# Moving the sub-norm's partition sum on GpSimd, and four smaller steps, in a hand-ordered decoder trunk

## Chip, cores and metric

The kernel runs on one core of one Trainium2 chip. The metric is the device time of one execution in microseconds, the median of several runs. TensorE (PE, with its weight loads as PEld), VectorE (DVE), ScalarE (ACT), GpSimd (POOL) and SyncE (SP) each work through a queue of their own, in order, and wait for each other with semaphores. DMAs are issued from SP, POOL and ACT.

## The reference

One layer of a decoder trunk, 1024 tokens of width 2048, all in float32. Cut to what matters here:

```python
hn = rmsnorm(h, norm_mix_g[i])
proj = hn @ w_in[i]
sb_q, sb_k, sb_v, sb_g, df_q, df_k, df_v, df_g = jnp.split(proj, split_at, axis=-1)
sb_out = stick_breaking_attention(...)          # 8 heads of 128: "SB"
dq, dk = partial_rope(df_q), partial_rope(df_k) # 8 heads of 2 x 64: "DF"
df_out = differential_attention(dq, dk, df_v, lam)
df_out = rmsnorm(df_out, subln_g[i], SUBLN_EPS) * (1.0 - lambda_init)   # the sub-norm, over 128 columns of a head
mixed = concat([sb_out * silu(sb_g), df_out * silu(df_g)])
h = h + mixed @ w_out[i]
gate = sigmoid(rmsnorm(h, norm_ple_g[i]) @ w_ple_gate[i])
h = h + gate * (p[i] @ w_ple_proj[i])
return rmsnorm(h, norm_final_g)
```

## The kernel before

Everything lies transposed: features on the 128 partitions, tokens along the free axis, in two halves of 512 tokens. Every large product is made with three matmuls, because an operand is split into a high part (a cast to fp32r, on ACT) and a low part (what is left, a subtraction on DVE): high x high, high x low and low x high. In the profile the high casts are lines such as L202, L517, L682, L684, L802 on ACT, and the low parts L198, L522, L688, L690, L816 on DVE.

The work comes in this order:

1. **The v and gate columns** of the input projection, as block products with seven multiplications (operands A11, A12, S1 to S4, A22, class `Seven`). One `prod` is 12 matmuls, and after each one `step` is called, which counts `slot` up by one. A step splits one more piece of weights (`whigh` L802, `wlow` L816), then does what is in `soon`, then calls `chore`, then takes up to two operand splits out of the list `xq` whose slot has come (three if more than eight wait, four after the change in slots of the new set `rush`). In `chore` there is also the dictionary `joint`: at given slots it sums the squares of x over partitions (`total`, GpSimd, L1152), takes the root (`root`, ACT, L1157 and L1158) and refines it in three DVE steps (`refined`, L1166, L1168, L1170), once for each token half.
2. **The q and k columns and both attentions.** For each token half (half 1 first, then half 0) and each of 16 heads, in the order DF, SB, DF, SB, ..., `unit` makes 96 matmuls, three for each of its 32 ticks. After each tick `side.tick()` runs those steps of a list sorted by due time that have come due. All of attention is in that list: scores, softmax or stick-breaking, transposes of the weights (`turn`, L498), their splits (`parts`: high part L516 and L517, low part L521 and L522), the products with v (`mix`, L540 and L543 to L545), the sub-norm of a DF head, and the turning of q and k of the head that was just projected. `side.later(dt, fn)` puts a step in dt ticks after the present one. Numbers come from the table `TICK`; heads 15 and 7 of each half have entries of their own under `mid_` (half 1) and `end_` (half 0).
3. **The output projection and the gate product**, again `Seven` (`op`), `gprod` being the version that calls `step` after each 12 of its 24 matmuls; `gate_loads` loads operands of the gate product and puts their splits into `xq`.

The orders of PE, DVE and ACT are the program's order, written by hand. The orders of SP and POOL are made by the scheduler when the kernel is built, from the program's order and a simulated timeline.

The sub-norm of a DF head, after its last product with v: `squared` (Square on ACT, L572, and the product with the sub-norm's gain on DVE, L573) three ticks after that `mix`, the sum over partitions on GpSimd (`partition_all_reduce`, L579) a tick and a half later, and at a fixed tick `norm`: Ln and Exp on ACT (L589, L590), four DVE steps (L593 to L596).

In the first half (half 1) a unit of an SB head looks like this, by the ticks of that unit: the last `mix` of the DF head before it at tick 6; Square at 9 and the partition sum at 10; the last addition of k's rotary turn (L1583) at 11, the four casts of k (L1560, L1564) at 14, its low parts (L1571) at 16 and 17, the casts into k's ends (L1578) at 18; meanwhile the first transposes of another SB head at tick 11 and their `mix` at 17, the next one at 23; Ln of the DF head's sub-norm at 26.

Of the kernel before, what the change touches and what calls it, by code (L numbers as in the profile page):

```python
# [19 lines left out]
ALU = mybir.AluOpType  # L20
# [22 lines left out]
TICK = {  # L43
    "neg": 2, "cs": 27, "x0_at": (7, 7, 8, 7), "end_df_soft": (1, 1.5, 4.5, 5.5), "df_inv": 4, "mid_df_inv": 2.7,
    "end_df_inv": 4.5, "sumlag": 2, "gvx": ((22, 27), (80, 85)), "chore": 86, "rows": 25, "opx": (8, 12), "turn": 76, "lag":
    15, "gap": (4, 6), "parts": (1, 2), "vparts": (2, 3), "sums": (0, 2), "squared": (3, 4.5), "norm": (1, 4), "df_scores":
    (-20, -16, -13, -8, -4, 0, 4, 8), "df_turn": (19, 19), "df_v": -15.5, "df_norm": 44.5, "sb_scores": (-2, 5.5, 13.5, 22),
    "sb_turn": (32, 36), "sb_v": 19, "df_soft": (1, 1.5, 4, 5.5), "sb_stick": (1, 1, 3, 5.5), "taken": (28, 31), "sb_split":
    (1, 2), "kv": 9, "df_vg": (20, 42, 58, 59.5), "sb_vg": (4, 16, 24, 25.5), "q_turn": (-1.0, 5.5, 5, 6.5, 10, 12,
# [22 lines left out]
def _body(ctx, nc, tc, ap):  # L72
# [7 lines left out]
    V, G, A, T = nc.vector, nc.gpsimd, nc.scalar, nc.tensor  # L80
# [6 lines left out]
    subg = const.tile([P, 1], F32, name="subg", tag="subg")  # L87
# [193 lines left out]
    side = Side()  # L281
# [67 lines left out]
    def attention(at, pz, half, hd, q, qz, K, KL, VV, sg, vg, rcol):  # L349
# [4 lines left out]
        def tk(nm):  # L354
            return TICK.get(seam + nm, TICK[nm])
# [11 lines left out]
        avs = {}  # L367
        wjs = {}
        sqs = {}
# [157 lines left out]
        def mix(pr, g):  # L527
            if g == 0:
                avs[pr] = pp.tile([P, 4, P], F32, name="av", tag="t")
            av4 = avs[pr]  # L530
            av = av4[:, 2:4, :].rearrange("p a b -> p (a b)")
            for j in range(2):
                blk = 2 * (pr + g) + j
                vv = VV[blk // 4]
                last = blk == nb - 1
                if blk == 2 * pr:


                    for i in range(2):
                        T.matmul(av4[:, 0:2, :], vv[:, i, blk % 4, :], wjs[pr, g][j], start=i == 0, stop=i == 1)  # L540
                    continue
                wh, wl = wjs[pr, g][j]
                T.matmul(av, vv[:, 0, blk % 4, :], wh, start=blk == 2 * pr + 1, stop=False)  # L543
                T.matmul(av, vv[:, 1, blk % 4, :], wh, start=False, stop=False)  # L544
                T.matmul(av, vv[:, 0, blk % 4, :], wl, start=False, stop=last)  # L545
            if not last:
                return
            ms_ = slice(pr * 2 * P, (pr + 1) * 2 * P)
            if sb:
                sm = ev.tile([P, 2, P], F32, name="sm", tag="sm", bufs=5)  # L550
            else:
                if pr == 0:
                    avs["both"] = ev.tile([P, 4, P], F32, name="avb", tag="ssq")
                sm = avs["both"][:, 2 * pr:2 * pr + 2, :]
            av = sm.rearrange("p a b -> p (a b)")
            side.later(tk("sums")[0], lambda: A.copy(sm[:, 1, :], av4[:, 3, :]))

            def summed():
                V.reduce_sum(sm[:, 0, :], av4[:, 0:3, :].rearrange("p a b -> p b a"), axis=AX.X)
                if sb:  # L560
                    V.tensor_tensor(sg[:, ms_], av, sg[:, ms_], op=ALU.mult)
                    if pr == 1:
                        mixed(half, hd, sg)

            side.later(tk("sums")[1], summed)
            if sb or pr == 0:
                return

            def squared():
                both = avs["both"].rearrange("p a b -> p (a b)")  # L570
                sq = ev.tile([P, HALF], F32, name="sqv", tag="xt", bufs=4)
                A.activation(sq, both, AF.Square)  # L572
                V.scalar_tensor_tensor(sg, both, subg[:, 0:1], sg, op0=ALU.mult, op1=ALU.mult)  # L573
                sqs[0] = both, sq

            def summed_squares():
                both, sq = sqs[0]
                msq = ev.tile([P, HALF], F32, name="msq", tag="xt", bufs=4)
                G.partition_all_reduce(msq, sq, P, RED.add)  # L579
                sqs[0] = both, sq, msq  # L580

            side.later(tk("squared")[0], squared)
            side.later(tk("squared")[1], summed_squares)

        def norm():
            rs_, t, msq = sqs[0]
# [22 lines left out]
        gap = tick("gap")[half]  # L609
# [23 lines left out]
    with tc.tile_pool(name="at", bufs=2) as at, tc.tile_pool(name="pz", bufs=2, space=PSUM) as pz:  # L633
# [23 lines left out]
        class Seven:  # L657

            def __init__(self, w, n):
                self.w = w  # L660
                self.units = [(ph, u) for ph in range(2) for u in range(n)]
                self.wq, self.XC, self.T = {}, {}, {}
                self.made, self.late, self.slot = [], 0, 0
                self.xq = deque()
                self.after = None
                self.soon, self.ended, self.free, self.calm = [], {}, {}, False
                self.extra, self.pause, self.ticks, self.chore = (), (), False, None

            def places(self, place, nm):
                where, t = place  # L670
# [164 lines left out]
            def step(self):  # L835

                self.slot += 1
                if self.slot not in self.pause:
                    self.whigh()
                    self.wlow()  # L840
                if self.slot in self.extra:
                    self.whigh()
                    self.wlow()
                self.due()
                if self.chore:
                    self.chore(self.slot)
                for _ in range(3 if len(self.xq) > 8 and not self.calm else 2):
                    e = next((e for e in self.xq if e[0] <= self.slot), None)
                    if e:
                        self.xq.remove(e)  # L850
                        e[1]()
# [10 lines left out]
        gv = Seven(lambda u, ph, k: ap["w_vg"][u, ph, k], NVG)  # L862
# [175 lines left out]
        def load_x(nm, i):  # L1038

            hi, lo = gv.places(PLACE[nm][i], nm)  # L1040
            ka, kb = KX[1][i]
            src = {"A11": (1, ka), "A12": (1, kb), "A22": (0, kb)}.get(nm)
            if src:
                raw = spare()
                with tc.issue_after(gv.lastw.ins):
                    nc.sync.dma_start(raw, xsrc(*src))
                return partial(gv.split, nm, i, hi, lo, gcol(src[1]), raw, True)
            nc.sync.dma_start(lo.bitcast(F32), xcomb_d[("S1", "S2", "S3", "S4").index(nm), i])
            return partial(gv.split, nm, i, hi, lo, gcol(ka) if nm == "S3" else None, None, True)
# [34 lines left out]
        def after(u, ph, nm):  # L1084
            if u < NVG - 1:
                return
            if ph == 0:
                gv.xq.extend((gv.slot + 2, load_x(nm, i)) for i in range(4))
            elif nm in ("S2", "S4"):
                gv.xq.extend((10 ** 9, load_x1(i + (4 if nm == "S4" else 0))) for i in range(4))  # L1090

# [64 lines left out]
        def root(hf):  # L1156
            A.activation(ssa[hf], totals[hf], AF.Ln, bias=eps6[:, 0:1], scale=1.0 / D)  # L1157
            A.activation(ssa[hf], ssa[hf], AF.Exp, scale=-0.5)  # L1158
            rstds[hf] = ssa[hf]

        def refined(hf, i):
            if i == 0:
                steps[hf] = ev.tile([P, HALF], F32, name="nt", tag="xt", bufs=4)
            t, ps, r = steps[hf], totals[hf], ssa[hf]
            if i == 0:
                V.scalar_tensor_tensor(t, ps, EPS * D, r, op0=ALU.add, op1=ALU.mult)  # L1166
            elif i == 1:
                V.scalar_tensor_tensor(t, t, -0.5 / D, r, op0=ALU.mult, op1=ALU.mult)  # L1168
            else:
                V.scalar_tensor_tensor(r, t, 1.5, r, op0=ALU.add, op1=ALU.mult)  # L1170
# [7 lines left out]
                rturned[hf] = const.tile([P, 4], F32, name=f"rturned{hf}", tag=f"rturned{hf}")  # L1178
                nc.sync.dma_start(rturned[hf], r_d[hf].rearrange("(j p) -> p j", p=P))

        joint = {71: partial(total, 1), 72: partial(total, 0), 75: partial(root, 1)}
        joint.update({76 + i: partial(refined, 1, i) for i in (0, 2)})
        joint[77] = lambda: (refined(1, 1), root(0))
        joint.update({79 + i: partial(refined, 0, i) for i in range(3)})
        joint[88] = consts_late
        joint[100] = turn_r

# [181 lines left out]

        def gate_loads(nm, i0, n=4, eng=nc.sync):  # L1370
            e = [(op.slot + (3 if nm in ("A11", "A12") else GLAT.get(nm, 2)), gate_operand(nm, i0 + j, eng)) for j in range(n)]
            if nm == "A11" and i0 > 3:
                xq.extendleft(reversed(e))
            else:
                xq.extend(e)
# [1104 lines left out]
```

## Time and profile before

| | |
|---|---|
| median of 3 runs | 2306.66 us (2305.09, 2306.66, 2309.38) |
| the profiled execution: time | 2306.0 us |
| the profiled execution: span | 2304.2 us |
| PE busy | 2276.3 us, 99% of the span, 10903 matmuls |
| DVE busy | 1828.9 us, 79% |
| ACT busy | 1326.4 us, 58% |
| POOL busy | 393.0 us, 17% |
| granted clock | 0.999 |

Busy time is the union of an engine's instructions. A matmul's end is modelled, so what PE lost is better read from the starts of its matmuls than from its busy share. In a timeline each row has the start, the duration, the engine, the line and the operands of an instruction (or of several like it in a row), and in brackets how long its engine was idle before it and what ended that.

### The profile page before, as it was taken

How to read it: one execution, taken by the hardware profiler on the slowest of the kernel's cores; microseconds unless marked ns; L12 is line 12 of the kernel's file. 1: busy time of each engine (PE TensorE's matmuls, PEld its weight loads, DVE VectorE, ACT ScalarE, POOL GpSimd, SP SyncE). 2: the span in 40 equal slices, each digit the busy share in tenths (PEclk: the TensorE clock that was granted, in tenths of full speed). 3: DMA queues.
4: the chain of work that ended last, by engine and by line, in shares of the span. 5: the costliest groups of instructions: out<-in, count | busy, mean ns of one | idle time of the engine just before them, and what ended most of it. 6: DMA issues, size and time to landing. Idle time of an engine off the chain costs nothing.

```text
span 2304.2 us, 32562 instructions
## 1 busy us (share of the span) xinstructions
PE 2276.3 (99%) x10903; PEld 1906.3 (83%) x10903; DVE 1828.9 (79%) x3135; ACT 1326.4 (58%) x2397; POOL 393.0 (17%) x520
## 2 busy tenths in 40 slices
PE   9999999999999999999999999999999999999998
PEld 7888888888888888887888888888888888888887
DVE  6588887777768888878778778778787988786887
ACT  6424354444467777778877777777733435542555
POOL 2121211111212222211021111121221121111100
PEclk9999999999999999999999999999999999999999
DMA  7698687876898878889687677787899789998975
GB/s 269 211 307 260 201 251 230 236 218 193 236 297 258 243 251 255 251 283 302 198 222 189 183 213 218 207 210 233 254 217 247 247 247 284 328 345 259 311 256 190
DMA packets 291260, 565.05 MB, mean 245 GB/s; under 512 B 63746, under 2 KB 74242, under 8 KB 291092
## 3 DMA queue, kind: packets, MB, share of 16 engines
q1 hardware_dynamic: 220276, 383.35, 52.7%
q0 software_dynamic: 58864, 158.10, 25.1%
q10 hardware_dynamic: 11952, 21.53, 2.6%
q8 instruction: 85, 1.39, 0.3%
q14 instruction: 83, 0.68, 0.1%
HBM read 359.17 MB, written 203.69 MB: 244 GB/s over the span
## 4 chain that ended last, share of the span: by engine, by line
PE 86%; DVE 7%; DMA 3%; issue 2%; ACT 2%; SPq 0%; DVEq 0%; ACTq 0%
PE pbc L707 13%; PE pa L707 9%; PE pc L707 9%; PE acc L297 9%; PE acc L299 9%; PE acc L298 9%; PE pb L707 4%; PE tp L498 2%; PE pb L1901 1%; PE pb L1902 1%; PE pb L1900 1%; PE z L390 1%; PE av L545 1%; PE z L389 1%; PE av L544 1%
## 5 line engine op out<-in xcount | busy, mean ns | idle before, releaser
L802 ACT CAST wpr<-T 128x512 fp32r<-128x512 f32 x208 | 127.6, 620 | 439.2 <-DVE T L761 365.3
L297 PE MATMUL acc<-xh,whi 128*128 128x512 f32 x768 | 309.9, 404 | 0.0
L299 PE MATMUL acc<-xh,wlo 128*128 128x512 f32 x768 | 300.4, 391 | 0.0
L298 PE MATMUL acc<-xl,whi 128*128 128x512 f32 x768 | 300.4, 391 | 0.0
L299 PEld LDWEIGHTS acc<-xh,wlo 128*128 128x128 f32 x768 | 144.2, 188 | 31.8
L297 PEld LDWEIGHTS acc<-xh,whi 128*128 128x128 f32 x768 | 144.7, 188 | 25.1 <-ACT qk L1529 0.2
L298 PEld LDWEIGHTS acc<-xl,whi 128*128 128x128 f32 x768 | 144.9, 189 | 24.2
L816 DVE TENSOR_TENSOR wpr<-T,wpr 128x512 fp32r<-128x512 f32 x208 | 147.8, 711 | 5.9 <-ACT wpr L802 5.2
L802 ACT CAST wpr<-wraw 128x512 fp32r<-128x512 f32 x128 | 78.7, 617 | 122.8 <-DMA wraw<-tw_d 36.7
L202 ACT CAST whi<-wraw 128x1024 fp32r<-128x1024 f32 x128 | 134.0, 1047 | 11.5 <-DMA wraw<-w_in 8.6
L522 DVE TENSOR_TENSOR awl<-tp,awh 128x256 fp32r<-128x256 f32 (+1 forms) x160 | 92.6, 579 | 35.3 <-ACT awh L517 34.7
L445 ACT ACTIVATE et<-z,mx 128x512 f32<-128x512 f32 (+7 forms) x128 | 95.0, 742 | 43.1 <-DVE mx L437 42.5
L707 PE MATMUL pbc<-cA,wpr 128*128 128x512 f32 x480 | 115.8, 390 | 1.2 <-DVE u L1246 1.1
L437 DVE CUSTOM_DVE_ANT_0 z<-z,wide 128x512 f32<-128x512 f32 (+7 forms) x128 | 97.6, 764 | 24.0 <-PE z L390 22.4
L707 PE MATMUL pc<-cS,wpr 128*128 128x512 f32 x480 | 115.3, 389 | 0.0
L707 PE MATMUL pbc<-cS,wpr 128*128 128x512 f32 x480 | 115.3, 389 | 0.0
L915 POOL DMA_DIRECT2D vg_d<-hc x96 | 62.5, 651 | 278.2 <-DVE hc L1141 146.4
L707 PEld LDWEIGHTS pbc<-cA,wpr 128*128 128x128 f32 x480 | 89.9, 188 | 21.1 <-DVE u L1246 2.5
L707 PEld LDWEIGHTS pc<-cS,wpr 128*128 128x128 f32 x480 | 90.1, 188 | 18.7
L707 PEld LDWEIGHTS pbc<-cS,wpr 128*128 128x128 f32 x480 | 90.1, 188 | 18.7
L707 PE MATMUL pbc<-cS2h,wpr 128*128 128x512 f32 x320 | 105.2, 390 | 0.0
L707 PE MATMUL pc<-cS4h,wpr 128*128 128x512 f32 x320 | 105.0, 389 | 0.0
(539 smaller groups left out, 6493.8 us busy)
## 6 DMA issues: line engine op xcount, KB each, us to landing
wraw<-w_in SPq DMA_DIRECT2D x128, 512.0 KB, 4.8
wraw<-w_vg SPq DMA_DIRECT2D x143, 256.0 KB, 3.9
wlo_d<-wlo POOLq DMA_DIRECT2D x56, 512.0 KB, 6.4
vg_d<-hc POOLq DMA_DIRECT2D x96, 256.0 KB, 4.4
wlo<-wlo_d SPq DMA_DIRECT2D x48, 512.0 KB, 3.9
wraw<-w_gate SPq DMA_DIRECT2D x92, 256.0 KB, 5.4
h_d<-hc POOLq DMA_DIRECT2D x56, 256.0 KB, 5.1
wraw<-w_out SPq DMA_DIRECT2D x56, 256.0 KB, 4.4
```

Of the source, the lines that this page charges most:

```text
L202: side.later(1, lambda: A.copy(hi[:, o], raw[:, o]))
L297: T.matmul(acc[c], hi[:, k2, kh, c, :], xh, start=first, stop=False)
L298: T.matmul(acc[c], hi[:, k2, kh, c, :], xl, start=False, stop=False)
L299: T.matmul(acc[c], lo[k2][:, kh, c, :], xh, start=False, stop=last)
L437: V.tensor_tensor_reduce(z[:, vw], z[:, vw], add, -DF_SCALE, 3.0e38, ALU.add, ALU.min, mx)
L445: A.activation(et[:, vw], z[:, vw], AF.Exp, bias=mx[:, 0:1], scale=-1.0, accum_out=l[:, c:c + 1])
L498: T.transpose(tp[:, j, b * P:(b + 1) * P], ws[2 * pr + b][:, (g0 + j) * P:(g0 + j + 1) * P], ident)
L522: V.tensor_tensor(wl[:, o, :], tp[:, o, :], wh[:, o, :].bitcast(F32), op=ALU.subtract)
L707: T.matmul(o, a[:, w], x, start=start and k + i == 0, stop=k == 3 and i == 2, skip_group_check=True)
L802: A.copy(t[:, 0], src)
L816: V.tensor_tensor(t[:, 1], src, t[:, 0].bitcast(F32), op=ALU.subtract)
L915: G.dma_start(vg_d[hf, blk, u], o, **(dict(accum_op=ALU.add) if ph else {}))
```

## The change

Five edits; no arithmetic is changed.

- The Square and the partition sum of the sub-norm become one step. In half 1 it is due 12.9 ticks after the last `mix` (3 for the `mid_` head), in half 0 three ticks after it. The product with the gain stays at three ticks.
- The splits of the first two tiles of the output projection's operand A11, in the last unit, are due later: tick 16.5 instead of 14, and 17 instead of 16.
- The splits of the third and fourth tile of S4, at the seam of the two phases of stage 1, may be taken at slot + 3 instead of slot + 2.
- `root` and `refined` of both halves are one slot earlier.
- When the last four tiles of the gate product's A22 are loaded, the slot two later takes four splits from the list instead of two.

```diff
-    15, ... "squared": (3, 4.5), "norm": (1, 4), ...
+    15, ... "squared": (3, 12.9), "mid_squared": (3, 3), "norm": (1, 4), ...
-    ... "A11": ((11.5, 14), (9.6, 16), (9.5, 21), (10.1, 23.5)), ...
+    ... "A11": ((11.5, 16.5), (9.6, 17), (9.5, 21), (10.1, 23.5)), ...
 
             def squared():
                 both = avs["both"].rearrange("p a b -> p (a b)")
+                V.scalar_tensor_tensor(sg, both, subg[:, 0:1], sg, op0=ALU.mult, op1=ALU.mult)
+
+            def summed_squares():
+                both = avs["both"].rearrange("p a b -> p (a b)")
                 sq = ev.tile([P, HALF], F32, name="sqv", tag="xt", bufs=4)
                 A.activation(sq, both, AF.Square)
-                V.scalar_tensor_tensor(sg, both, subg[:, 0:1], sg, op0=ALU.mult, op1=ALU.mult)
-                sqs[0] = both, sq
-
-            def summed_squares():
-                both, sq = sqs[0]
                 msq = ev.tile([P, HALF], F32, name="msq", tag="xt", bufs=4)
                 G.partition_all_reduce(msq, sq, P, RED.add)
                 sqs[0] = both, sq, msq
 
-            side.later(tk("squared")[0], squared)
-            side.later(tk("squared")[1], summed_squares)
+            side.later(3, squared)
+            side.later(tk("squared")[half], summed_squares)
...
+                self.rush = set()
...
-                for _ in range(3 if len(self.xq) > 8 and not self.calm else 2):
+                for _ in range(4 if self.slot in self.rush else 3 if len(self.xq) > 8 and not self.calm else 2):
...
-                gv.xq.extend((gv.slot + 2, load_x(nm, i)) for i in range(4))
+                gv.xq.extend((gv.slot + (3 if nm == "S4" and i > 1 else 2), load_x(nm, i)) for i in range(4))
...
-        joint = {71: partial(total, 1), 72: partial(total, 0), 75: partial(root, 1)}
-        joint.update({76 + i: partial(refined, 1, i) for i in (0, 2)})
-        joint[77] = lambda: (refined(1, 1), root(0))
-        joint.update({79 + i: partial(refined, 0, i) for i in range(3)})
+        joint = {71: partial(total, 1), 72: partial(total, 0), 74: partial(root, 1)}
+        joint.update({75: partial(refined, 1, 0), 76: lambda: (refined(1, 1), root(0)), 77: partial(refined, 1, 2)})
+        joint.update({78 + i: partial(refined, 0, i) for i in range(3)})
...
+            if nm == "A22" and i0:
+                op.rush.add(op.slot + 2)
```

More of the change, by code (lines that the diff above doesn't have):

```diff
@@ L45 @@
     "end_df_inv": 4.5, "sumlag": 2, "gvx": ((22, 27), (80, 85)), "chore": 86, "rows": 25, "opx": (8, 12), "turn": 76, "lag":
-    15, "gap": (4, 6), "parts": (1, 2), "vparts": (2, 3), "sums": (0, 2), "squared": (3, 4.5), "norm": (1, 4), "df_scores":
+    15, "gap": (4, 6), "parts": (1, 2), "vparts": (2, 3), "sums": (0, 2), "squared": (3, 12.9), "mid_squared": (3, 3), "norm": (1, 4), "df_scores":
     (-20, -16, -13, -8, -4, 0, 4, 8), "df_turn": (19, 19), "df_v": -15.5, "df_norm": 44.5, "sb_scores": (-2, 5.5, 13.5, 22),
```

2 rows, old and new, of the table TICK are left out of this document.

## The prediction

> **What bounds the kernel now.** I read the page first (engines, chain), then the waits of PE, then the timelines of the places where PE waits.
>
> ```profile
> span 2304.2 us, 32562 instructions
> PE 2276.3 (99%) x10903; PEld 1906.3 (83%) x10903; DVE 1828.9 (79%) x3135; ACT 1326.4 (58%) x2397; POOL 393.0 (17%) x520
> PE 86%; DVE 7%; DMA 3%; issue 2%; ACT 2%; SPq 0%; DVEq 0%; ACTq 0%
> ```
>
> PE is the bound, and the change takes no matmul away. So only PE's idle time can be gained, 2304.2 - 2276.3 = 28 us by the modelled ends, start and end of the kernel included. The waits of PE, first those from 690 to 1050 us (the first half of attention), then from 1570 to 1700 us, then from 100 to 500 us:
>
> ```profile
> PE av L540 <- DVE lead L521: 7.8, 7, 1.5
> PE av L545 <- DVE awl L522: 3.2, 6, 1.4
> PE pbc L707 <- DVE u L1246: 1.1, 2, 0.9
> ```
>
> The seven waits for `lead` are one event that recurs with each of the seven DF heads of the first half outside the `mid_` seam. One of them on PE, ahead of it the same stretch of work without a wait in the other half, for comparison:
>
> ```profile
> 1578.39 0.39 PE L299 MATMUL acc<-xh,wlo 128*128 128x512 f32 x1
> 1579.57 0.48 PE L297 MATMUL acc<-xh,whi 128*128 128x512 f32 x1
> ...
> 759.18 0.40 PE L299 MATMUL acc<-xh,wlo 128*128 128x512 f32 x1
> 760.63 0.50 PE L540 MATMUL av<-lead,v 128*128 128x256 f32 x2 [1.05 <-DVE lead L521]
> 761.68 0.47 PE L297 MATMUL acc<-xh,whi 128*128 128x512 f32 x1
> ```
>
> From the L299 to the L297 behind the same five products and four transposes it is 1.18 us undisturbed and 2.50 us here: one such wait costs 1.32 us, not the 1.05 in the bracket, since ends are modelled. Why `lead` is late, on POOL, ACT and DVE:
>
> ```profile
> 754.73 3.54 POOL L579 PARTITION_ALL_REDUCE msq<-sqv  x1 [4.05 <-ACT sqv L572]
> 754.00 0.63 ACT L572 ACTIVATE sqv<-avb 128x512 f32<-128x512 f32 x1
> 757.85 0.62 ACT L1560 CAST k<-qk 64x512 fp32r<-64x512 f32 x1 [1.12 <-DVE qk L1583]
> 755.41 2.41 DVE L1583 TENSOR_TENSOR qk<-qk,sw 128x512 f32<-128x512 f32 x1
> 757.74 1.21 DVE L198 TENSOR_TENSOR wlo<-wraw,whi 128x1024 fp32r<-128x1024 f32 x1
> 760.31 0.27 DVE L521 TENSOR_TENSOR lead<-tp,lead 128x128 fp32r<-128x128 f32 x1
> L1583 DVE TENSOR_TENSOR qk<-qk,sw x32: 656/682/2614, 645.2 to 1573.8; 128x512 f32<-128x512 f32 x32
> ```
>
> L1583 has a median of 0.68 us but takes 2.41 when it starts 0.68 us into the partition sum on GpSimd. Both of its inputs are in SBUF. It behaves as if held until 757.14 (its end less 0.68), 2.4 us into the sum. That is 1.73 us lost on DVE, and DVE runs without a gap from there to `lead`, which ends at 760.58; PE goes on 0.05 us later.
>
> **The change part by part.**
>
> *The partition sum, first half.* Without Square ahead and the sum beside it, L1583 ends at 756.09 and the same DVE queue comes to `lead` 1.73 us earlier: it ends at 758.85. PE wants it one matmul (0.23 us) after 759.18, at 759.41. So the wait goes, with 0.5 us to spare, and what is next on PE's list has to be looked for at the new place. Square is now due at tick 18 of the unit, behind the four casts L1560/L1564, the casts into k's ends and a high part of the transposes:
>
> ```profile
> 761.96 0.59 ACT L517 CAST awh<-tp 128x512 fp32r<-128x512 f32 x1 [0.50 <-PE tp L498]
> 762.44 0.61 ACT L1578 CAST k<-kl 64x128 fp32r<-64x128 f32 x2
> 769.56 0.72 ACT L589 ACTIVATE avb<-msq,eps 128x512 f32<-128x512 f32 x1
> 766.35 0.28 PE L545 MATMUL av<-awl,v 128*128 128x256 f32 x1
> 779.68 1.22 DVE L198 TENSOR_TENSOR wlo<-wraw,whi 128x1024 fp32r<-128x1024 f32 x1
> ```
>
> With PE 1.32 us earlier L517 starts at about 760.65, the four L1578 follow (0.31 each) to 762.4, Square ends at 763.0, and the sum runs from 763.1 to 766.6. What DVE has then: the second L198 from 760.9 (behind the two L1571) to 762.1, the low part L522 to 762.8, two short masks to 763.3, a scan and a product over 127 columns. L198 and L522 are done before the sum starts; PE's next need is that L522, at 766.35 - 1.32 = 765.0, 2.2 us later. The scan and product may lose the 1.73 us, but their transposes come at the unit's last tick. On ACT, L589 reads the sum at about 769.56 - 1.32 = 768.2, 1.6 us after its end. On POOL the sum now stands ahead of the stores of k, k's low part and the next low weights; all go to memory that half 0 reads hundreds of microseconds later, and the low weights' buffer is written again only by the row at 779.68, over 10 us after that store could be issued. So six heads give 6 x 1.32 = 7.9 us. The seventh head is just ahead of the seam:
>
> ```profile
> 1032.18 2.61 DVE L1583 TENSOR_TENSOR qk<-qk,sw 128x512 f32<-128x512 f32 x1
> 1036.19 0.39 PE L299 MATMUL acc<-xh,wlo 128*128 128x512 f32 x1
> 1038.11 0.50 PE L540 MATMUL av<-lead,v 128*128 128x256 f32 x2 [1.53 <-DVE lead L521]
> ```
>
> It loses 1038.11 - 1036.19 - 0.23 = 1.69 us; DVE gives back 1.93, but ACT also has x splits there, so I take 1.2 to 1.7, with 1.5. Together 9.4 us. Bounds: nothing, if an equal wait arises at the new place, and 9.6 if all seven vanish.
>
> The Trainium skill (SBUF — State Buffer, Who interferes with whom) says that a DVE instruction with two SBUF inputs contends with a GpSimd instruction that reads SBUF, and that the second to issue "fully blocks" for the whole instruction, while one with at most one SBUF input does not. The trace agrees that it is a two-input operation that is held, but shows it released 2.4 us into a sum of 3.54, not at its end. By the rule's length the sum at its new place would cost 3.5 us to any two-input subtraction that arrives late; that is the second rival below.
>
> *The partition sum, second half and `mid_`.* Square keeps its tick, the sum's tick is 1.5 earlier in program order but waits for Square as before: the rows of the sum start 0.1 us after Square's end. 0 us; bounds +-0.5, the part of one POOL issue (0.53 to 0.68).
>
> *A11 in the last unit.*
>
> ```profile
> 1579.99 0.60 ACT L682 CAST cA11h<-cA11l 128x512 fp32r<-128x512 f32 x1
> 1580.63 2.40 DVE L688 TENSOR_TENSOR cA11l<-cA11l,cA11h 128x512 fp32r<-128x512 f32 x1 [1.09 <-ACT cA11h L682]
> 1584.38 0.69 DVE L522 TENSOR_TENSOR awl<-tp,awh 128x512 fp32r<-128x512 f32 x1
> 1585.12 0.38 PE L545 MATMUL av<-awl,v 128*128 128x256 f32 x1 [1.39 <-DVE awl L522]
> 1587.12 1.49 DVE L420 TENSOR_TENSOR_SCAN pt<-pt 128x639 f32<-128x639 f32 x1 [0.92 <-ACT pt L413]
> ```
>
> Here the operand's low part is caught by the sum (it takes 2.40 for 0.69) and stands ahead of L522, which PE awaits. At tick 18 (where both new due times fall) the two subtractions stand behind L522, as in the other heads of this half, where no wait for L522 shows. PE wanted to start this L545 0.12 us after the L544 at 1583.45, at 1583.57; it started 1.55 us later. Gain 1.55. The two subtractions and casts (2 x 0.69 on DVE, 2 x 0.6 on ACT) then stand ahead of the masks and sigmoids of the next scores; DVE idles 0.92 us there now, before the scan at 1587.12, which covers most of the 1.38. So I take 1.5, with bounds 0.2 (both subtractions pass on in full) and 1.6.
>
> *A22 at the start of the last stage.*
>
> ```profile
> 2185.04 0.72 ACT L684 ACTIVATE cgA22h<-cgA22l,gvec 128x512 fp32r<-128x512 f32 x1 [0.61 <-DMA cgA22l<-h_d]
> 2190.46 0.62 ACT L802 CAST wpr<-wraw 128x512 fp32r<-128x512 f32 x1 [4.09 <-DMA wraw<-tw_d]
> 2192.04 1.32 ACT L684 ACTIVATE cgA22h<-cgA22l,gvec 128x512 fp32r<-128x512 f32 x2
> 2193.50 1.41 DVE L690 SCALAR_TENSOR_TENSOR cgA22l<-cgA22l,gvec,cgA22h 128x512 fp32r<-128x512 f32 x2
> 2194.30 0.50 PE L1901 MATMUL pb<-cgA22l,wpr 128*128 128x512 f32 x1 [0.63 <-DVE cgA22l L690]
> ```
>
> The last pair of casts (2192.04) stands behind L802, which waits 4.09 us for weights. With four taken a slot earlier, each pair moves up one step, and the last one stands ahead of that wait, at about 2186.5. The price is on ACT at 2185.04: these casts wait for their own loads, and L802 of the next step waits behind them for 3 us, which the idle 4.09 covers. PE's matmul before that L1901 starts at 2193.28; it lost 2194.30 - 2193.28 - 0.23 = 0.79 us. Gain 0.8, bounds 0 and 0.8.
>
> *S4 and the roots.*
>
> ```profile
> 323.41 1.29 ACT L682 CAST cS4h<-cS4l 128x512 fp32r<-128x512 f32 x2 [0.25 <-DMA cS4l<-xcomb_d]
> 327.67 1.14 ACT L682 CAST cS4h<-cS4l 128x512 fp32r<-128x512 f32 x2
> 299.46 0.69 DVE L1141 TENSOR_TENSOR hc<-pbc,s 128x512 f32<-128x512 f32 x1 [1.43 <-PE pbc L707]
> 330.27 3.03 PE L707 MATMUL pbc<-cA,wpr 128*128 128x512 f32 x12 [0.90 <-DVE u L1246]
> ```
>
> Only two splits are taken in a step, so the third and fourth S4 tile already come a slot after the first two (323.41 and 327.67 are a step apart). The S4 edit changes no order: 0 us. The first refining step moves into the 1.43 us in which DVE waits at 299.46, so DVE's backlog up to 320 us is 0.6 us (one such operation) shorter, and with it the load that delays 327.67 and so u3. Gain 0.5 of the 1.06 us lost at 330.27; bounds -0.5 and 1.
>
> Sum: 9.4 + 0 + 1.5 + 0.8 + 0.5 = 12.2 us. Some of it will be lost where DVE is busy without a gap, as before the waits of 1.1 to 1.3 us at the seam of the halves; I take 0.7 off: 11.5. The profiled execution took 2306.0 us (span 2304.2), 0.7 below the median of 2306.66. 2306.0 - 11.5 = 2294.5; I keep that for the median.
>
> **The rivals.**
>
> 1. *Part of it moves.* The sum holds up DVE at its new place and PE waits at tick 23 or at the seam. For it: the sum still takes 3.5 us and ACT reaches Square only by my reckoning. Against it: 2.2 us of slack where the loss is 1.73. If half of the 9.4 comes back, 2306.0 - (4.7 + 2) = 2299.
> 2. *The stretch is moved whole*, each head losing again what it gained; the others give 2.8 - 0.7 = 2: 2304, within 0.2%. It needs Square 1 to 2 us earlier than I have it, so that L198 is caught, and a hold as long as the sum.
> 3. *Slower: the sum comes too late for Ln.* ACT works in order; if L589 waits for the sum, the exponentials and casts behind it wait too, and PE with them. Slack 1.6 us. It decides where POOL puts the sum behind stores: three of them (0.68 + 0.55 + 0.53) add 1.8 us and just use it up. To end 4.6 us slower the seven heads would have to lose (11.5 + 4.6) / 7 = 2.3 us each, the sum 4 us late: about 2311.
> 4. *The change doesn't do what it says*: true of S4, as shown; and POOL's and SP's orders are made anew at the build, which could move a load by a few us either way.
>
> **How the numbers follow.** About 0.2% (4.6 us) is what a measurement of this kernel can tell from no change. Forecast as worked out: 0.70, own range 2291 to 2297.5. Rival 1: 0.16. Rival 2 with the order effects of 4: 0.10. Rival 3: 0.04. Faster: forecast and rival 1, and a little of the rest: 0.87; same 0.09; slower 0.04. The range takes in rival 1 and the upper part of what lies between it and rival 2: 2291 to 2303.
>
> **What would show it.** Right: no row of PE waiting for `lead` between 690 and 1050 us; L1583 at 0.68 in all heads; the sum some 8 us later in its unit; no wait at 1585 or in the first A22 product; cS4h casts in pairs as before. Wrong: waits of L543 or L545 for `awl` at tick 23 of SB units, L589 idle until the sum, L198 stretched, or larger waits at the seam of the halves that take back what the seven heads gave.

## The result, and the profile after

| | before | after |
|---|---|---|
| median | 2306.56 us, 6 runs (2305.09 to 2309.38) | 2293.07 us, 6 runs (2292.20 to 2294.83) |
| profiled execution: time, span | 2306.0, 2304.2 us | 2292.35, 2290.6 us |
| granted clock | 0.999 | 0.999 |

The ratio is 0.9942, 95% interval 0.9929 to 0.9955: faster by 13.5 us (0.6%), 1.4 us more than forecast (2294.5) and inside its range.

The page of the kernel after, the span and the engines:

```profile
span 2290.6 us, 32565 instructions
PE 2273.1 (99%) x10903; PEld 1906.8 (83%) x10903; DVE 1825.6 (80%) x3135; ACT 1326.7 (58%) x2397; POOL 390.8 (17%) x520
```

PE's idle time by these ends went from 28 to 17.5 us. Its busy time fell 3.2 us with the same 10903 matmuls; their ends are modelled, and a matmul behind a wait is written down longer (0.50 for 0.40 us). So starts are what counts below.

The waits of PE from 690 to 1062 us in the kernel after, with the total, the number and the longest. That is all of them:

```profile
PE z L389 <- ACT et L445: 1.5, 1, 1.5
PE av L540 <- DVE lead L521: 1.3, 1, 1.3
PE tp L498 <- DVE et L460: 0.6, 1, 0.6
```

The seven waits for `lead` in the heads are gone; all three that are left lie at the seam, where half 1 passes into half 0, from 1045 us on. The same head as in the prediction, in the timelines of POOL, ACT, DVE and PE of the kernel after (the turn of k, L1583 before, is now L1584; Square L576, the sum L578, Ln L588):

```profile
756.55 0.68 POOL L1504 DMA_DIRECT2D k_d<-k  x1 [1.33 <-ACT k L1565]
758.29 0.55 POOL L1506 DMA_DIRECT2D kl_d<-kl  x1 [1.05 <-DVE kl L1572]
759.54 0.53 POOL L199 DMA_DIRECT2D wlo_d<-wlo  x1 [0.71 <-DVE wlo L198]
760.28 3.23 POOL L578 PARTITION_ALL_REDUCE msq<-sqv  x1 [0.20 <-DMA wraw<-w_in]
...
759.55 0.63 ACT L576 ACTIVATE sqv<-avb 128x512 f32<-128x512 f32 x1
765.41 0.72 ACT L588 ACTIVATE avb<-msq,eps 128x512 f32<-128x512 f32 x1
...
752.57 0.69 DVE L1584 TENSOR_TENSOR qk<-qk,sw 128x512 f32<-128x512 f32 x1
755.75 0.26 DVE L521 TENSOR_TENSOR lead<-tp,lead 128x128 fp32r<-128x128 f32 x1
759.16 0.69 DVE L522 TENSOR_TENSOR awl<-tp,awh 128x512 fp32r<-128x512 f32 x1
760.88 1.91 DVE L420 TENSOR_TENSOR_SCAN pt<-pt 128x127 f32<-128x127 f32 x1 [0.50 <-ACT pt L413]
...
756.36 0.39 PE L299 MATMUL acc<-xh,wlo 128*128 128x512 f32 x1
756.58 0.40 PE L540 MATMUL av<-lead,v 128*128 128x256 f32 x2
```

The turn of k takes 0.69 us again, `lead` ends at 756.01, and PE goes from L299 to L540 in 0.22 us without a wait. The sum still costs DVE time: it now holds the scan L420, that is, stretches it to 1.91 us where the kernel before has it at 0.42, but no product is waiting for that scan. POOL put the sum behind three stores, not ahead of them, and it lost nothing by that: it starts 0.10 us after Square's end. (The bracket of its row names a load of weights, which the sum doesn't read; Square's end is what it follows, by 0.1 to 0.2 us in each of the seven heads.)

To see which place gave what, I compared each matmul's start with the start of the same matmul in another kernel (the order on PE is the same). The table has the time from the first matmul after one point to the first after another, in us; the points are times of the profile of before.

| stretch of before | before | S4 alone | sum alone | A11 alone | roots alone | A22 alone | after | after, second profile |
|---|---|---|---|---|---|---|---|---|
| 325 to 340 | 15.05 | 14.30 | 14.17 | 15.35 | 13.62 | 14.13 | 13.62 | 13.64 |
| 700 to 1040 | 339.98 | 339.76 | 330.31 | 340.04 | 340.02 | 339.98 | 330.30 | 330.56 |
| 1040 to 1062 | 22.02 | 21.98 | 22.22 | 21.99 | 21.99 | 21.99 | 22.40 | 22.46 |
| 1580 to 1590 | 9.91 | 9.92 | 9.92 | 8.27 | 9.91 | 9.91 | 8.27 | 8.28 |
| 1590 to 1630 | 40.11 | 39.16 | 39.16 | 41.19 | 39.17 | 39.17 | 39.15 | 39.15 |
| 1630 to 1650 | 20.08 | 19.65 | 19.82 | 20.10 | 19.87 | 19.66 | 19.66 | 19.77 |
| 1780 to 1830 | 50.09 | 50.09 | 50.09 | 50.09 | 50.32 | 50.09 | 50.67 | 50.09 |
| 1940 to 1960 | 19.98 | 19.95 | 19.95 | 20.80 | 19.95 | 19.95 | 20.44 | 19.95 |
| 2180 to 2200 | 19.95 | 20.55 | 20.55 | 19.83 | 20.61 | 19.04 | 19.04 | 19.04 |
| 2250 to 2310 | 45.06 | 46.20 | 46.44 | 45.06 | 45.06 | 45.06 | 45.06 | 45.06 |

S4 alone has the very order of before on every engine. So where these two columns differ, by up to 1.1 us, it is one execution against another and nothing else. That is the scale for every row.

### The profile page after: what moved, and what is told of

Its sections match the earlier page's. It is cut to its first block, busy times and chain, and to the rows that moved or that the text cites. A ratio compares the mean times of both kernels' runs of the same rounds, so it can differ in the third digit from the quotient of the medians.

```text
span 2290.6 us, 32565 instructions
## 1 busy us (share of the span) xinstructions
PE 2273.1 (99%) x10903; PEld 1906.8 (83%) x10903; DVE 1825.6 (80%) x3135; ACT 1326.7 (58%) x2397; POOL 390.8 (17%) x520
## 4 chain that ended last, share of the span: by engine, by line
PE 90%; issue 4%; DVE 3%; ACT 1%; DMA 1%; POOL 1%; DVEq 0%; POOLq 0%; SPq 0%; ACTq 0%
PE pbc L707 12%; PE acc L297 10%; PE acc L299 10%; PE acc L298 10%; PE pa L707 9%; PE pc L707 8%; PE pb L707 4%; PE tp L498 3%; PE pb L1902 2%; PE pb L1901 2%; PE pb L1903 2%; PE av L545 1%; PE z L390 1%; PE z L389 1%; PE av L544 1%
## 5 line engine op out<-in xcount | busy, mean ns | idle before, releaser
L297 PE MATMUL acc<-xh,whi 128*128 128x512 f32 x768 | 309.9, 404 | 0.0
L299 PE MATMUL acc<-xh,wlo 128*128 128x512 f32 x768 | 300.4, 391 | 0.0
L299 PEld LDWEIGHTS acc<-xh,wlo 128*128 128x128 f32 x768 | 144.2, 188 | 31.5
L297 PEld LDWEIGHTS acc<-xh,whi 128*128 128x128 f32 x768 | 144.6, 188 | 25.2 <-ACT qk L1530 0.2
L522 DVE TENSOR_TENSOR awl<-tp,awh 128x256 fp32r<-128x256 f32 (+1 forms) x160 | 92.7, 579 | 35.3 <-ACT awh L517 34.8
L420 DVE TENSOR_TENSOR_SCAN pt<-pt 128x511 f32<-128x511 f32 (+3 forms) x64 | 95.9, 1498 | 20.2 <-ACT pt L413 19.6
```

Of the source, the lines that this page charges most:

```text
L297: T.matmul(acc[c], hi[:, k2, kh, c, :], xh, start=first, stop=False)
L299: T.matmul(acc[c], lo[k2][:, kh, c, :], xh, start=False, stop=last)
L420: V.tensor_tensor_scan(pt[:, w], pt[:, w], pt[:, w], initial=1.0, op0=ALU.mult, op1=ALU.bypass)
L522: V.tensor_tensor(wl[:, o, :], tp[:, o, :], wh[:, o, :].bitcast(F32), op=ALU.subtract)
```

## The experiments

The theory: GpSimd's partition sum holds a DVE operation with two inputs in SBUF for 2 us and more, and costs PE whatever stands behind that operation and is awaited. Moved to where DVE has nothing PE needs soon, it costs nothing. Rivals: the gain came from Square's place on ACT; any later place would have served; the small edits made it, or the orders that the build made anew.

**The sum's edit alone.**

```diff
-"squared": (3, 4.5)
+"squared": (3, 12.9), "mid_squared": (3, 3)
...      # Square goes into summed_squares, ahead of the sum, as in the change
-            side.later(tk("squared")[0], squared)
+            side.later(3, squared)
+            side.later(tk("squared")[half], summed_squares)
```

> The kernel before with the first edit alone: Square and partition sum 12.9 ticks after the mix in the first half. Theory (the sum holds back two-input DVE operations, 1.73 us a head, and PE pays 1.3 to 1.8 us for each of seven heads): the seven waits for lead between 690 and 1050 us are gone, L1583 takes 0.68 us everywhere there, and the time falls by 9.3 to 9.9 us, to about 2297, less at most 0.5 us lost at the seam of the halves. Rival (the gain of the whole change comes mostly from the four smaller edits or from SP's and POOL's new orders): less than 6 us.

2296.56 us (2295.47 to 2299.49) against 2306.55 in the same series, ratio 0.9962 (0.9949 to 0.9974). The heads' stretch (700 to 1040 us) gets 9.67 us shorter, as in the full change, and the seam 0.2 longer. This edit is some three quarters of the result.

**The S4 edit alone.**

```diff
-gv.xq.extend((gv.slot + 2, load_x(nm, i)) for i in range(4))
+gv.xq.extend((gv.slot + (3 if nm == "S4" and i > 1 else 2), load_x(nm, i)) for i in range(4))
```

> The kernel before with the S4 edit alone. Prediction's step: no order changes, so the time is that of before within 1.5 us, and the wait of about 0.9 us at 330 us stays. Rival (the edit moves the third and fourth S4 split and so removes the wait at 330 us): 1.0 to 1.4 us faster.

2305.44 us, ratio 1.0000 (0.9991 to 1.0009). No instruction of any engine stands elsewhere. Its use was as a second profile of the kernel before.

**Square early, the sum late.** Square stays at its old tick and only the sum is due later.

```diff
+"late": 12.9
...
-            side.later(tk("squared")[1], summed_squares)
+            side.later(TICK["late"] if half and not seam else tk("squared")[1], summed_squares)
```

> As e1_sum, but Square stays on ACT at its old tick, ahead of k's casts; only the partition sum on GpSimd is due 12.9 ticks after the mix. Theory (GpSimd's sum holds DVE): the waits for lead are gone as in e1_sum, the time is within 1.5 us of it, about 2297. Rival (Square's 0.54 to 0.63 us on ACT delays the casts and the chain behind them): the waits stay and the time is near 2306.

2306.5 us, ratio 1.0000 (0.9991 to 1.0009). Its DVE and POOL in the head shown above:

```profile
753.99 3.54 POOL L579 PARTITION_ALL_REDUCE msq<-sqv  x1 [4.04 <-ACT sqv L572]
...
754.66 2.41 DVE L1583 TENSOR_TENSOR qk<-qk,sw 128x512 f32<-128x512 f32 x1
```

The sum ran right behind Square as before. The order of the instructions is that of before on POOL, ACT, DVE and PE, POOL had been idle for 4.04 us, and a due time in the program makes no engine wait. So my expectation was wrong, and the run does not part Square from the sum, as it was meant to. What it shows is that a later tick for the sum alone doesn't move it: it runs when Square is done, so the change had to move Square.

**An idle sum at the old place.** The sum's edit, and a second sum over the head's averages where the old one was. Nothing reads it.

```diff
...      # tiles() takes the two buffers of the real sum
+            def idle_sum():
+                tiles()
+                G.partition_all_reduce(sqs[1][1], avs["both"].rearrange("p a b -> p (a b)"), P, RED.add)
+            if half and not seam:
+                side.later(4.5, idle_sum)
```

> As e1_sum, and in each of the seven heads GpSimd also makes a second partition sum at the old place, of the attention output itself into a tile that nobody reads then; Square and the real sum are late. Theory: the idle sum starts about 2 us earlier than the old one did (it doesn't wait for Square) and holds another two-input operation of DVE ahead of lead for 1.5 to 2 us, so the waits for lead are back, 1.0 to 1.6 us each, and the time is 2304 to 2309. Rival (it was ACT's Square, or the order of the queues): no waits, about 2297.

2307.41 us, ratio 1.0006 (0.9997 to 1.0015): all of the gain is gone. POOL, DVE and PE in the same head:

```profile
751.84 3.60 POOL L587 PARTITION_ALL_REDUCE msq<-avb  x1 [2.00 <-DVE avb L559]
...
752.25 2.74 DVE L571 SCALAR_TENSOR_TENSOR sg<-avb,subg,sg 128x512 f32<-128x512 f32 x1
759.73 0.27 DVE L521 TENSOR_TENSOR lead<-tp,lead 128x128 fp32r<-128x128 f32 x1
764.86 1.70 DVE L420 TENSOR_TENSOR_SCAN pt<-pt 128x127 f32<-128x127 f32 x1 [0.49 <-ACT pt L413]
...
760.05 0.50 PE L540 MATMUL av<-lead,v 128*128 128x256 f32 x2 [1.13 <-DVE lead L521]
```

Square is at the new tick here, and PE waits for `lead` all the same, in all seven heads. It is the sum alone, and it doesn't matter which two-input operation it catches: here it is the product with the gain, 2.74 for 0.75 us. The rival of Square on ACT falls.

**Square and the sum in between.** The sum's edit alone, with another tick.

```diff
-"squared": (3, 12.9)
+"squared": (3, 6.9)
```

> The kernel before with the sum's edit alone, but Square and the sum due at 6.9 and not 12.9 in the first half, so that the sum runs from about 754.5 and holds what DVE has ahead of lead. Theory (what counts is which two-input operation of DVE, ahead of a product that PE awaits, falls 0.4 us or more into the sum): the waits for lead stay at 1 us or more in the six heads and the time is 2305 to 2307. Rival (any place behind the turn of k serves, since that is the operation held before): waits gone, 2297.

2305.59 us against 2305.81, ratio 0.9999 (0.9990 to 1.0008). Not every later place serves. Five of the seven heads wait for `lead`, 1.5 us each, more than before; two don't, one of them among the six of which I expected it. By the starts 0.9 us is gained in the heads' stretch, and 0.4 lost again at the seam. One of each kind, POOL, DVE and PE, first at 757 us and then at 813 us:

```profile
757.52 3.18 POOL L578 PARTITION_ALL_REDUCE msq<-sqv  x1
757.41 2.84 DVE L420 TENSOR_TENSOR_SCAN pt<-pt 128x255 f32<-128x255 f32 x1
760.17 0.26 DVE L521 TENSOR_TENSOR lead<-tp,lead 128x128 fp32r<-128x128 f32 x1
760.49 0.51 PE L540 MATMUL av<-lead,v 128*128 128x256 f32 x2 [1.48 <-DVE lead L521]
...
813.37 3.61 POOL L578 PARTITION_ALL_REDUCE msq<-sqv  x1
813.26 0.69 DVE L420 TENSOR_TENSOR_SCAN pt<-pt 128x255 f32<-128x255 f32 x1
813.87 0.27 DVE L521 TENSOR_TENSOR lead<-tp,lead 128x128 fp32r<-128x128 f32 x1
814.05 0.41 DVE L522 TENSOR_TENSOR awl<-tp,awh 128x256 fp32r<-128x256 f32 x1
814.38 1.89 DVE L424 TENSOR_TENSOR bt<-pt,bt 128x255 f32<-128x255 f32 x1
814.69 0.40 PE L540 MATMUL av<-lead,v 128*128 128x256 f32 x2
```

In both heads the scan starts 0.11 us ahead of the sum. In one it is caught and `lead` behind it is late; in the other it runs free, `lead` is in time and the product L424 *behind* `lead` is caught instead (1.89 for 0.41 us). The sum's own length tells which of the two came first: 3.18 us where it held the scan, 3.61 where the scan ran free, to 0.58 us into the sum. PE pays only where the held operation stands ahead of the one that it awaits.

The orders made anew by the build don't explain the gain: of SP's 1265 transfers three stand elsewhere in the sum's edit alone, and three in this run, which gains nothing by its time.

**An idle sum of a quarter of the columns.** As the idle sum above, over 128 columns.

```diff
+                G.partition_all_reduce(sqs[1][1][:, 0:P], avs["both"].rearrange("p a b -> p (a b)")[:, 0:P], P, RED.add)
```

> The kernel before with the sum's edit and an idle sum at the old place, as in the run with an idle sum, but over 128 columns instead of 512. Nothing reads the idle sum. Theory: what holds a two-input operation of DVE is the sum's work, so the hold shrinks with it; a sum of a quarter of the columns lasts about 1 us, and lead, with 0.5 us of slack, is late by 0.2 us at most: 2296 to 2298. Rival: the hold is a fixed price of starting a sum there (2.4 us as with 512 columns), the waits of 1.1 us come back: 2306 or more.

2296.68 us, ratio 0.9960 (0.9948 to 0.9973), the time of the sum's edit alone. But its first 128 columns are ready earlier, and the idle sum ran at 740.66, 11 us ahead of the old place, so the time says nothing of `lead`, for which the run was made. POOL and DVE there, and in the seventh head:

```profile
740.66 1.35 POOL L587 PARTITION_ALL_REDUCE msq<-avb  x1
...
741.23 1.30 DVE L420 TENSOR_TENSOR_SCAN pt<-pt 128x511 f32<-128x511 f32 x1 [0.16 <-ACT pt L413]
...
1010.76 1.07 POOL L587 PARTITION_ALL_REDUCE msq<-avb  x1 [3.19 <-DVE avb L559]
1010.77 1.05 DVE L1525 TENSOR_TENSOR sg<-sg,gf 128x512 f32<-128x512 f32 x1
```

What remains is a reading of the hold. The scan starts 0.57 us into the sum and takes 1.30 us, where the kernel with the sum's edit alone has 1.22; with 512 columns a scan that started 0.60 us into the sum lost 1.49. In the seventh head the product L1525 starts 0.01 us into the sum and takes 1.05 us for its usual 0.68. So the hold shrinks with the sum.

**A11 alone.**

```diff
-"A11": ((11.5, 14), (9.6, 16), ...
+"A11": ((11.5, 16.5), (9.6, 17), ...
```

> The kernel before with the due times of A11 in the last unit of its first two entries alone (14 to 16.5, 16 to 17). Theory: the low-part subtraction of A11 that the sum held for 2.40 us goes behind L522, the wait of 1.39 us at 1585.12 goes, and the idle DVE before the scan takes up the two subtractions: 1.5 us off, about 2305.0. Rival: the same wait comes back at the next product or at the masks and sigmoids behind them, then 0 to 0.3 us, about 2306.4. All other waits stay, those for lead too.

2304.90 us (2302.28 to 2307.13), ratio 0.9992 (0.9983 to 1.0001): by its time it can't be told from no change. By the trace the wait at 1585.12 is gone and 1.64 us with it (9.91 to 8.27). DVE there:

```profile
1581.38 0.69 DVE L522 TENSOR_TENSOR awl<-tp,awh 128x512 fp32r<-128x512 f32 x1
1582.59 2.01 DVE L688 TENSOR_TENSOR cA11l<-cA11l,cA11h 128x512 fp32r<-128x512 f32 x2 [0.52 <-ACT cA11h L682]
1586.06 1.49 DVE L420 TENSOR_TENSOR_SCAN pt<-pt 128x639 f32<-128x639 f32 x1 [0.92 <-ACT pt L413]
```

L522 stands ahead of the two subtractions. The sum still holds these (2.01 for 1.4 us), but the scan behind them waits 0.92 us for ACT as it did before: they found room in idle time. Its profile has 1.05 and 0.82 us more at 1626 and 1947 us, where no instruction's order differs.

**The second 1/rms alone.**

```diff
-joint = {71: partial(total, 1), 72: partial(total, 0), 75: partial(root, 1)}
+joint = {71: partial(total, 1), 72: partial(total, 0), 74: partial(root, 1)}
...      # the refining steps one slot earlier too
```

> The kernel before with the second 1/rms and its refining steps one step earlier, alone. The prediction gave 0.5 us of the 1.06 lost at 330.27; the changed kernel shows the place 1.17 us earlier and the next one (333.70) another 0.20. Theory now: the whole loss at 330.27 was one step of DVE's backlog, so 1.2 to 1.4 us off by this edit alone, about 2305.2. Rival: the gain there came with the sum's edit through other transfers, then 0 to 0.5 here.

2304.56 us (2303.83 to 2306.68), ratio 0.9995 (0.9987 to 1.0004). The stretch from 325 to 340 us is 13.62, in all five profiles with the edit 13.62 to 13.65. Without it, it is 14.13 to 14.30 in seven kernels, 15.05 in the profile of before and 15.35 in that of A11. So the edit gives 0.5 to 0.7 where the place is undisturbed, and the profile of before had 0.75 to 0.9 more there by chance. My expectation of 1.2 to 1.4, read from one pair of profiles, mixed the two.

**A22 alone.**

```diff
+            if nm == "A22" and i0:
+                op.rush.add(op.slot + 2)     # four splits taken in that slot
```

> The kernel before with the fourth A22 load taken in one slot, alone. Theory: the last pair of casts stands ahead of the cast that waits 4 us for weights, and the 0.8 us lost at 2194.30 go: about 2305.7, at the edge of what can be told. Rival: the earlier loads delay a load of weights on the same queue and PE loses as much at another step of that stage: 0. In the changed kernel two later places came out 0.49 and 0.46 us worse (its 1786.85 and 1934.26, in the last stages); if this edit makes them, they show here.

2305.50 us (2302.86 to 2308.09), ratio 0.9996 (0.9987 to 1.0005). ACT at the place:

```profile
2182.59 0.72 ACT L685 ACTIVATE cgA22h<-cgA22l,gvec 128x512 fp32r<-128x512 f32 x1 [2.38 <-DMA cgA22l<-h_d]
2184.99 1.33 ACT L685 ACTIVATE cgA22h<-cgA22l,gvec 128x512 fp32r<-128x512 f32 x2
2189.13 0.62 ACT L803 CAST wpr<-wraw 128x512 fp32r<-128x512 f32 x1 [2.21 <-DMA wraw<-tw_d]
```

The last pair of casts stands ahead of the cast that waits for weights, and PE has no wait left from 2170 to 2200 us. With the edit the stretch is 19.04 in all five profiles that have it. Without it, it is 19.83 to 20.61, so it is worth 0.8 to 1.6.

**The kernel after once more, and two versions beside it**, one series, before at 2305.86 (2304.28 to 2308.19).

> The changed kernel once more, beside the versions below on one chip, for two things. First, between 1780 and 1830 us and between 1940 and 1960 us its first profile had 0.58 and 0.49 us more than that of before. Theory: these are weights and stores landing at other times, which change from one execution to the next, as 325 to 340 and 1590 to 1650 us did among kernels with the same order there; then a second profile has other values at these places, and the six heads, 1585, the first A22 product and the seam are as before. Rival: the change makes them, then both come again within 0.1 us. Second, the measure for the next two: about 2293.

2292.64 us (2291.78 to 2292.88), ratio 0.9943 (0.9930 to 0.9957). The extra 0.58 and 0.49 us at 1800 and 1947 are gone in its profile, and 0.5 us has come at 1684: execution to execution, as the theory had it. The first version moves the scaling of the rotation tables:

```diff
-    "neg": 2, "cs": 27,
+    "neg": 2, "cs": 50,
```

> The changed kernel with one due time more: the scaling of the rotation tables (1.22 us of DVE ahead of the refining steps at the seam, at 1038.98) at unit tick 50 and not 27. Theory: DVE is busy without a gap from there to the maxima and lead that PE waits for (1.46 us at 1045.30, 1.33 at 1048.76), so both together fall by about 1.2 us and the time is 2292. Rival: the waits at the seam are set by ACT's exponentials or by loads, then 2293 and the waits stay.

2291.49 us (2290.41 to 2292.72), ratio 0.9939 (0.9927 to 0.9952). PE at the seam, the kernel after and then this version:

```profile
1045.30 0.44 PE L389 MATMUL z<-k,q 128*128 128x384 f32 x1 [1.46 <-ACT et L445]
```

```profile
1044.28 0.44 PE L389 MATMUL z<-k,q 128*128 128x384 f32 x1 [0.24 <-ACT et L445]
```

The wait falls by 1.22 us and the median by 1.15; the wait for `lead` behind it stays at 1.33. The ranges of the two overlap, but the trace shows the place. This version is the fastest with a mechanism shown. The second version has this edit and one more:

```diff
-                if seam == "mid_" and not sb:
-                    G.tensor_copy(words[:, :, :, c], planes[:, c])
-                else:
-                    A.copy(words[:, :, :, c], planes[:, c])
+                A.copy(words[:, :, :, c], planes[:, c])
```

> The version with the scaling moved, and the two copies of v's words at the seam on ACT and not on GpSimd. Theory: the refining step and the product that take 1.08 us instead of 0.69 there are held by those copies on GpSimd (1040.87, 2.41 us), and ACT idles 1.49 us at 1043.80, so another 0.3 to 0.8 us off the waits at the seam: 2291.5. Rival: the two copies on ACT (about 1.3 us by casts of the size) delay the exponentials behind them and PE loses 0.5 or more: 2293 or above.

2291.48 us (2290.29 to 2293.24), ratio 0.9939 (0.9926 to 0.9951): nothing more. POOL and DVE at the seam in the first version, then DVE, ACT and PE in this one:

```profile
1039.84 2.43 POOL L477 COPY vw<-vf 128x512 uint16<-128x512 uint16 x2 [4.26 <-DVE sqv L592]
1040.54 1.08 DVE L594 SCALAR_TENSOR_TENSOR avb<-sqv,avb 128x512 f32<-128x512 f32 x1
1041.66 1.09 DVE L595 TENSOR_TENSOR sg<-sg,avb 128x512 f32<-128x512 f32 x1
```

```profile
1040.18 0.69 DVE L591 SCALAR_TENSOR_TENSOR avb<-sqv,avb 128x512 f32<-128x512 f32 x1
1040.90 0.69 DVE L592 TENSOR_TENSOR sg<-sg,avb 128x512 f32<-128x512 f32 x1
...
1043.14 1.38 ACT L476 COPY vw<-vf 128x512 uint16<-128x512 uint16 x2
1044.39 0.57 ACT L1527 COPY qk<-acc 128x512 f32<-128x512 f32 x1
...
1045.02 0.50 PE L297 MATMUL acc<-xh,whi 128*128 128x512 f32 x1 [1.01 <-ACT qk L1527]
```

Both halves of the expectation are there: the two held operations are down from 1.08 to 0.69 us, and the two copies now stand on ACT ahead of the copy that frees PE's accumulator, for which PE waits 1.01 us. One pays for the other: the stretch at the seam (1040 to 1062 us) takes 21.40 us, 0.3 more than in the first version.

## Why the prediction was right

**The sum, first half.** Predicted 6 x 1.32 and 1.5 for the seventh head, 9.4; measured, from L299 to L297, 1.30 to 1.33 in six heads and 1.78 in the seventh, and 9.67 for the stretch. The reckoning of the place held: moved by the 2.82 us that the kernel had gained by then in earlier places (L299 from 759.18 to 756.36), the predicted start of 763.1 is 760.28, and the sum starts at 760.28. L522 ends 0.43 us before the sum starts, the scan is caught (+1.49 us) and no product of PE waits for it. Two parts of the step were off without effect. POOL's order puts the sum behind three stores, which rival 3 had feared; they were done 0.1 us before Square's end let the sum start, and Ln reads the sum 1.9 us after its end, where I had 1.6, since the sum takes 3.23 us at the new place and not 3.5. The seventh head gave 0.1 above its upper bound of 1.7.

**Rival 1 and rival 2**, that the held time reappears in front of PE, did not happen here. The run with the sum in between shows what rival 2 feared: there the sum starts 5.0 us earlier against the L299 ahead of the wait (1.1 us before it, not 3.9 us behind it), and nothing of the gain is left by its time. But rival 2's own condition, Square 1 to 2 us earlier "so that L198 is caught", was not run, and the operation caught was another (the scan L420).

**What is held, and how long.** In the run with the sum in between, L522 (one input in PSUM) runs 0.68 us into a sum at its usual 0.41, and the next operation, L424 (both inputs in SBUF), is held. In the run with Square early L1583 ends at 757.07, the sum at 757.53: less its own 0.69 us it was released 2.4 us into a sum of 3.54. The Trainium skill (SBUF — State Buffer, Who interferes with whom) says that operations with two SBUF inputs contend with a GpSimd instruction that reads SBUF, which agrees, and that the later of the two is blocked for the whole instruction of the first, which does not: the held operation ends before the sum does. Nor does a scan that started 0.11 us *ahead* of the sum and was still held fit an order by recorded starts. The 2.4 us of that row is no constant either. In the profiles of all these runs, taking an operation's usual time off its end, the two-input operations held by a sum of 512 columns were released 2.0 to 2.6 us into it, and always 1.1 to 1.2 us ahead of its recorded end. What varies is the front of the sum: it takes 3.2 us where no operation with two SBUF inputs is running on DVE when it starts, and where one is, 3.0 to 3.1 us from that operation's end on (3.54 us in the head of the prediction, where the subtraction L1569 ends 0.43 us into it). So by these spans each of the two waits for the other. Spans on GpSimd are rough, so where in the sum the release lies is as the profile records it.

**A11.** 1.5 predicted, 1.64 measured. **A22.** 0.8 predicted, 0.91 against the profile of before. **S4.** 0, as predicted.

**The roots.** 0.5 predicted, 0.5 to 0.7 by the kernels with and without the edit. In the pair before and after alone the place gives 1.43 (15.05 to 13.62), because the profile of before was worse there than seven other kernels without the edit.

**What the terms add up to.** Against the median before, 2306.66, the forecast of 2294.5 is a gain of 12.2 us. The medians differ by 13.5, in the second series by 13.2, and the interval of the ratio runs from 10.4 to 16.4 us, so the times alone show no term to be wrong. By the starts the edits are worth 9.7 + 1.6 + 0.8 to 1.6 + 0.5 to 0.7 - 0.4 at the seam, together 12.2 to 13.2, where the prediction had 11.5: A22 was low by up to 0.8, the sum by 0.3, and the 0.7 taken off for losses behind the gains came out at 0.4. One part of the hit is luck: the 11.5 was taken off the profiled time and set against a median 0.7 above it, which gives the 0.7 back.

I also read the profile of before as typical, and its waits at 330, 1626 and 1643 us were not: 0.75 to 0.9, 0.95 and 0.2 to 0.4 us above most kernels with the same orders there (A11's profile has them too). The profiled pair shows 13.65 us, these in it. Of the one at 1626, ACT in the profile of before and of S4 alone, the same instruction and the same order:

```profile
1625.23 0.59 ACT L1628 COPY hc<-pa 128x512 f32<-128x512 f32 x1 [2.99 <-DMA part_d<-hc]
```

```profile
1622.18 0.59 ACT L1628 COPY hc<-pa 128x512 f32<-128x512 f32 x1 [1.17 <-DMA part_d<-hc]
```

By the profile the copy waits for a store to land, 2.99 us in one execution and 1.17 in the other. What makes that store late was not found.

## What to carry over

The long GpSimd instruction beside DVE had no price of its own here: look at which two-input DVE operation starts during it, and whether a product of PE stands behind that operation. A shift of a few microseconds was worth all or next to nothing. On an otherwise idle engine it was not the due time that placed the sum but its last input, so move the producer. Before pricing a wait of one microsecond that ends with a transfer, take a second profile of the same program: here the same order of instructions gave places that differ by up to 1.1 us, and an edit worth less shows in the trace's starts when its median shows nothing.

## What was not expected of the hardware

The hold is not decided by recorded starts alone: a scan that starts 0.11 us ahead of the sum is held to 2.84 us in one head and runs in 0.69 in another. The sum's length shows which it was, 3.18 and 3.61 us: the sum is held too, by a two-input operation that got in ahead of it. The hold ends before the sum does, 1.1 to 1.2 us ahead of the recorded end of every sum of 512 columns (3.2 to 3.7 us) that held an operation, and 0.7 us ahead of that of one of 128 columns (1.07 us). A sum takes no longer for an operation with one input in PSUM: with L2177, which reads PSUM, running until 0.50 us into it, it took 3.23 us. Two copies of 128x512 words on GpSimd (2.43 us for both) hold two DVE operations to 1.08 us instead of 0.69, much less than a sum does.
